# Hybrid encoder step: step sizes beside attention, one pool for LayerNorm and RG-LRU, gates ahead in the down stage

## The chip, the cores and the metric

One core of a Trainium2 chip runs the whole kernel. The metric is the device time of one execution in microseconds (us), a median of several. TensorE multiplies, VectorE (DVE), ScalarE (ACT) and GpSimd (POOL) do the rest, and every DMA is issued from one queue, that of SyncE (SP).

## The reference, cut to what matters

1088 frames (1024 of a new stream, 64 of a running one) go through one layer. One projection feeds four branches, their gates and four merge gates.

```
h = rms_norm(x); P = h @ w_in                       # 1088 x 1024 @ 1024 x 10248
A: RG-LRU:  conv4 -> r, i = sigmoid(block gates);  log_a = -8 r softplus(-lam)
            h_t = a_t h_{t-1} + sqrt(1 - a_t^2) (i_t x_t)
B: SSD:     conv4 -> SiLU; dt = softplus(P_dt + bias); chunked scan with decay exp(cumsum(-dt exp(a_log)))
C: conv31 over a GLU -> LayerNorm over channels -> swish
D: stick-breaking attention, 8 heads, strictly causal
u_b = branch_b * silu(gate_b);  y_b = u_b @ w_down[b];  m = sum_b sigmoid(P_merge_b) * y_b
x <- x + rms_norm(m @ w_out)
```

## The kernel before

Everything is in fp32 accuracy: each large product is three matmuls (`mm3`: high by high, high by low, low by high part), the parts made by `split` (a copy on ACT, a subtraction on DVE). `with tc.manual_schedule(engines={PE})` makes TensorE's order that of the source. The order on the other engines and on the DMA queue is set by the framework's planner: it takes what is ready by its own reckoning, the earlier in the source first, and `tc.high_priority(offset=...)` moves an instruction ahead. In a queue nothing passes a waiting instruction.

The stages, in order of time:

1. Norm of x, transposes to `hh`, `hl` (both parts of h, transposed, kept in SBUF).
2. Attention, L526 to L571: 4 head pairs `c`, 17 `Unit`s each (`scores`, `turn`, `output`). Between units `feed.step` puts pieces of projection chunks (`proj`: 24 matmuls into a PSUM tile `pj`, then `evac`). In the last head pair the chunks left in `extra` (15 pieces) are fed, at `want = 18 * (k + 1) // 16` pieces by unit k, so the last units have none.
3. T stage, L575 to L674. The gates of branch C (`spill`, 12 pieces, evacuated by ACT at L599) fill TensorE. Beside it the sums and differences of quarters of h are made for a Strassen-like product: `g11`..`g21` by eight `G.tensor_tensor` (POOL, L616), then differences on DVE (L618 to L624) and splits into `quad` 5, 6, 7 (and 4 at the end, over `hh`, `hl`). The step sizes of B are in this stage too: 48 matmuls with 16 columns of weights (L634), nine transposes (L640), softplus (L257) and the decay sums (L655).
4. Strassen stage, L720: 20 `Pair`s of chunks, 7 products each in `ORDER = (1, 2, 6, 5, 7, 3, 4)`, 24 matmuls each into PSUM tiles `bank` (6). After each product `next(side)` lets one step of the side chain issue its work: `layer_norm` (27 steps), then `lru` (35), then `ssd` (77), 139 of the 140 steps. Each opens its pool at its start, in the place of the one that it follows. `lru` handles 8 pieces (4 channel blocks, 2 halves of 544 frames): 6 + 6 matmuls a step apart, four sigmoids, Exp, Tanh, Sqrt, a scan, a split `uah`, `ual` and its stores. `uah` shares the memory of `ga`, the result of Exp, and `ual` that of `lg_t`, the gate that is loaded.
5. Down stage, L1114 to L1186: for each branch in `order = (3, 0, 2, 1)` and each of 8 column blocks d, pieces of 12 matmuls go to `pj3` (6 tiles), and DVE multiplies by the merge gate (L1165). The gate is loaded from `mgs` and goes through a sigmoid on ACT (`load_gate`, L1133). In the source the loads of the first operand (L1106, four) come first, then the first weights, then the second operand's four loads, then the eight gates. The tiles `mt` are placed ahead of the gates' tiles.
6. Output product, norm and store.

PSUM is one pool per stage group: `ps` (stages 1 to 3), `ps2` (4), `ps3` (5, 6). A pool with `reuse_waits="tile"` waits for the tiles that lay where its own tiles lie; without it, a new pool waits for all of the pools whose place it takes. The three PSUM pools have it not.

Of the kernel before, what the change touches and what calls it, by code (L numbers as in the profile page):

```python
# [8 lines left out]
FT = mybir.dt.float32  # L9
FR = mybir.dt.float32r  # L10
# [35 lines left out]
def encoder_step(ctx, tc, x, prm, win, wdt, wdn, wout, lwa, lwx, ckT, cv_, ssd0, npre, npost, dtb, alog, dskip,  # L46
# [10 lines left out]
    ps = ps1.enter_context(tc.tile_pool(name="ps", bufs=1, space=PSUM))  # L57
# [467 lines left out]

    feed.add(cf_sig(0), cf_glu(0), k_chunk(0), q_chunk(0), g_chunk(0))  # L526
# [7 lines left out]
    NU = 17  # L534
    units[0].scores()
    for m, u in enumerate(units):
        c, k = divmod(m, NU)
        if k == 0:
            if c < 3:
                feed.add(cf_sig(c + 1), v_chunk(c + 1) if c else extra.pop(0), extra.pop(0), g_chunk(c + 1), cf_glu(c + 1), extra.pop(0))  # L540
            else:
                feed.add(*extra)
            fed = 0
# [3 lines left out]
        want = min(18, 18 * (k + 1) // (NU - 1))  # L547
# [19 lines left out]
        else:  # L567
# [7 lines left out]
    wdr = const.tile([128, 8, 8], FT, name="wdr")  # L575
    dma(wdr, wdt)
    wd2 = const.tile([128, 8, 16], FR, name="wd2")
    S.activation(wd2[:, :, 0:8], wdr, AF.Copy)
    V.tensor_sub(wd2[:, :, 8:16], wdr, wd2[:, :, 0:8].bitcast(FT))
    dtb_t = const.tile([128, 8], FT, name="dtb_t")  # L580
    dma(dtb_t, ap(dtb, 0, [[0, 128], [1, 8]]))
    a_t = const.tile([128, 8], FT, name="a_t")
    dma(a_t, ap(alog, 0, [[0, 128], [1, 8]]))
    S.activation(a_t, a_t, AF.Exp)
    dsk = const.tile([128, 4], FT, name="dsk")
    for h in range(2):
        dma(dsk[h * 64:h * 64 + 64, :], ap(dskip, h, [[0, 64], [2, 4]]))
# [15 lines left out]
    feed.add(*(spill(C_CG + c, cg_d[:, c]) for c in range(4)))  # L603
    feed.step(1)
# [21 lines left out]
    feed.step(2)  # L626


    dtr = tmp.tile([16, T], FT, name="dtr")
    for i, (t0, n) in enumerate(SPL):  # L630
        p = pg()
        for k in range(8):
            for q, hx in enumerate((hh, hl)):
                PE.matmul(p[:16, :n], wd2[:, k, :], hx[:, k, t0:t0 + n], start=k == 0 and q == 0, stop=k == 7 and q == 1)  # L634
        S.activation(dtr[:, t0:t0 + n], p[:16, :n], AF.Copy)
    feed.step(3)
    pd = pg()
    for i in range(9):
        r = 128 if i < 8 else 64
        PE.transpose(pd[:r, i * 16:i * 16 + 16], dtr[:, i * 128:i * 128 + r], ident[:16, :16])  # L640
    pd3 = pd[:, :144].rearrange("p (i c) -> p i c", c=16)
    zb = tmp.tile([128, 9, 8], FT, name="zb", bufs=1)
    V.memset(zb, 0.0)
    for r, i0, i1 in ((128, 0, 8), (64, 8, 9)):
        V.tensor_tensor(zb[:r, i0:i1], pd3[:r, i0:i1, 0:8], dtb_t[:r, None, :].to_broadcast([r, i1 - i0, 8]), op=OP.add)
        V.tensor_tensor(zb[:r, i0:i1], pd3[:r, i0:i1, 8:16], zb[:r, i0:i1], op=OP.add)
    dt = dq.tile([128, 9, 8], FT, name="dt", bufs=1)
    V.tensor_copy(dt, softplus(tmp, zb, [9, 8], "spd"))
    adt = dq.tile([128, 9, 8], FT, name="adt", bufs=1)
    V.scalar_tensor_tensor(adt, dt, -1.0, a_t[:, None, :].to_broadcast([128, 9, 8]), op0=OP.mult, op1=OP.mult)  # L650
    V.memset(adt[64:128, 8, :], 0.0)
    feed.step(4)
# [25 lines left out]
    ps = ps2.enter_context(tc.tile_pool(name="ps2", bufs=1, space=PSUM))  # L678
# [84 lines left out]

    def layer_norm():
        lnp = ExitStack()
        ln = lnp.enter_context(tc.tile_pool(name="ln", bufs=1, side="right", reuse_waits="tile"))

# [13 lines left out]
        for q in range(4):  # L781
# [32 lines left out]
    def lru():
        p4 = ExitStack()
        lp = p4.enter_context(tc.tile_pool(name="lru", bufs=1, side="right", reuse_waits="tile"))
        nl = lp.tile([128, 4], FT, name="nl")
        V.tensor_scalar(nl, P("lam", 0, 4), -1.0, None, op0=OP.mult)
        sp = softplus(lp, nl, [4], "spl")
        lm8 = lp.tile([128, 4], FT, name="lm8")  # L820
        lp4 = lp.tile([128, 4], FT, name="lp4")
        V.tensor_scalar(lm8, sp, -8.0, None, op0=OP.mult)
        V.tensor_scalar(lp4, sp, 4.0, None, op0=OP.mult)
        hfin = lp.tile([128, 2, 4], FT, name="hfin")
        raws = [lp.tile([128, 128], FT, name=f"bd{e}") for e in "ax"]
        for r_ in raws:
            G.memset(r_, 0.0)

        def load(c, j):
            t = slice(j * HT, j * HT + HT)  # L830
            if j == 0:
                self.bd = []
                for r_, src, e in zip(raws, (lwa, lwx), "ax"):
# [3 lines left out]
                    self.bd.append([lp.tile([128, 128], FR, name=f"bd{e}{f}") for f in "hl"])  # L837
                    split(*self.bd[-1], r_)
            xc = lp.tile([128, HT], FT, name="xl", bufs=2)
            dma(xc, xl_d[:, c, t])  # L840
            xh, xl = (lp.tile([128, HT], FR, name=f"xg{f}") for f in range(2))
            split(xh, xl, xc)
            return xc, xh, xl

        class self:
            pass
        todo = [(c, j) for c in range(4) for j in range(2)]
        nxt = load(0, 0)
        yield from wait(3)
        for m, (c, j) in enumerate(todo):  # L850
            t = slice(j * HT, j * HT + HT)
            xc, xh, xl = nxt
            g = lp.tile([128, HT], FT, name="lg_t")
            dma(g, lg_d[:, c, t])
            gr = lp.tile([128, HT], FT, name="gr", bufs=2)
            gx = lp.tile([128, HT], FT, name="gx", bufs=2)
            for t0 in (0, QT):
                for dst, w, bias in ((gr, self.bd[0], P("ba", c)), (gx, self.bd[1], P("bx", c))):
                    p = pg()[:, :QT]
                    mm3(p, w[0], w[1], xh[:, t0:t0 + QT], xl[:, t0:t0 + QT], True, True)  # L860
                    S.activation(dst[:, t0:t0 + QT], p, AF.Sigmoid, bias=bias)
                if t0 == 0:
                    yield
            if m < 7:
                nxt = load(*todo[m + 1])
            ga = lp.tile([128, HT], FT, name="ga")
            S.activation(ga, gr, AF.Exp, scale=lm8[:, c:c + 1])  # L867
            S.activation(gr, gr, AF.Tanh, scale=lp4[:, c:c + 1])
            S.activation(gr, gr, AF.Sqrt)
            V.tensor_tensor(gx, gx, xc, op=OP.mult)  # L870
            V.scalar_tensor_tensor(gr, ga, 1.0, gr, op0=OP.add, op1=OP.mult)
            V.tensor_tensor(gx, gx, gr, op=OP.mult)
            hp_, hs = hfin[:, 0, c:c + 1], hfin[:, 1, c:c + 1]
            n = TP - HT if j else HT
            V.tensor_tensor_scan(gx[:, :n], ga[:, :n], gx[:, :n], hp_ if j else 0.0, OP.mult, OP.add)
            V.tensor_copy(hp_, gx[:, n - 1:n])
            if j:
                V.tensor_tensor_scan(gx[:, n:], ga[:, n:], gx[:, n:], P("h0", c), OP.mult, OP.add)
                V.tensor_copy(hs, gx[:, HT - 1:HT])
            V.tensor_tensor(gx, gx, g, op=OP.mult)  # L880
            uh = lp.tile([128, HT], FR, name="uah", tag="ga")
            ul = lp.tile([128, HT], FR, name="ual", tag="lg_t")
            split(uh, ul, gx)
            dma(uh_d[0][:, c, t], uh.bitcast(FT))
            dma(ul_d[0][:, c, t], ul.bitcast(FT))
            yield from wait(3)
        for i in range(2):
            dma(lh_o[i], hfin[:, i, :])
        p4.close()


    def ssd():
# [136 lines left out]
        yield from wait(3)  # L1029
# [244 lines left out]
```

## Time and profile before

| | us |
|---|---|
| median of 3 runs | 1481.57 (1480.87 to 1486.69) |
| profiled execution, its own time | 1485.84 |
| its span, first to last instruction | 1484.1 |
| TensorE busy with matmuls | 1421.5 |
| VectorE, ScalarE, GpSimd busy | 1065.9, 672.6, 266.4 |
| mean granted TensorE clock | 0.982 |

A row of the waits says which instruction waited for which, in total, how often and the longest. A row of the windows says how long each engine was busy in a stretch, with the instructions in brackets, and the granted TensorE clock as a share of 2.4 GHz (0.50 is 1.2 GHz).

### The profile page before, as it was taken

To read this page: it belongs to the slowest core of one execution; us is meant where nothing else is said; L and a number is where in the kernel's file an instruction comes from. 1 tells how busy PE (TensorE), PEld (TensorE's weight loads), DVE (VectorE), ACT (ScalarE), POOL (GpSimd) and SP (SyncE) were. 2 spreads that over 40 slices of the span, in tenths; PEclk is the share of its full clock that TensorE was granted. 3 is DMA by queue.
4 is the path that set the end of the run, shared out by engine and by line. 5 is a ranking of instruction groups with operands and counts; after the bars stand their busy time and mean duration, and the time that the engine had idled before them with its cause. 6 is when DMAs were issued, how large, how long until landed. Compare 5 with 4: busy or idle time off the path is not lost.

```text
span 1484.1 us, 25423 instructions
## 1 busy us (share of the span) xinstructions
PE 1421.5 (96%) x9901; PEld 1359.9 (92%) x9901; DVE 1065.9 (72%) x1628; ACT 672.6 (45%) x1225; POOL 266.4 (18%) x245
## 2 busy tenths in 40 slices
PE   8999999999999999899979989999999799999997
PEld 7999999999999998799979989999999799999885
DVE  6299799789779986847967775777877336668433
ACT  6224544544453464345769762443444242234211
POOL 0003221230231224513213231321211000000000
PEclk9999999999999999999999999999999989999999
DMA  6232213213213133134645444334343985643322
GB/s 216 69 88 65 71 49 90 94 41 101 76 55 93 52 102 107 53 109 146 207 138 175 156 139 140 124 108 154 121 132 97 334 336 170 242 149 101 112 86 71
DMA packets 113336, 184.45 MB, mean 124 GB/s; under 512 B 22080, under 2 KB 70080, under 8 KB 112704
## 3 DMA queue, kind: packets, MB, share of 16 engines
q1 hardware_dynamic: 113216, 182.82, 37.9%
q8 instruction: 78, 1.28, 0.4%
q14 instruction: 42, 0.34, 0.1%
HBM read 118.00 MB, written 60.59 MB: 120 GB/s over the span
## 4 chain that ended last, share of the span: by engine, by line
PE 38%; DVE 8%; DMA 5%; ACT 4%; issue 2%; SPq 0%; DVEq 0%; ACTq 0%
PE bank L736 16%; PE pj L109 6%; PE pj L111 6%; PE pj L110 6%; DVE w_lo L236 2%; DMA uh<-uoh 1%; DMA w_raw<-in_wout_dram 1%; DMA uh<-uah 1%; ACT w_hi L235 1%; DMA sga<-mgs 1%; PE pg L927 1%; DVE r L743 1%; PE pg L980 1%; DVE lnx L802 1%; ACT L867 1%
## 5 line engine op out<-in xcount | busy, mean ns | idle before, releaser
L110 PE MATMUL pj<-hl,w_hi 128*128 128x384 f32 (+4 forms) x1184 | 384.3, 325 | 1.1 <-DVE hl L232 1.1
L109 PE MATMUL pj<-hh,w_hi 128*128 128x384 f32 (+4 forms) x1088 | 354.4, 326 | 6.0 <-ACT t L599 4.6
L111 PE MATMUL pj<-hh,w_lo 128*128 128x384 f32 (+4 forms) x1088 | 351.9, 323 | 0.0
L110 PEld LDWEIGHTS pj<-hl,w_hi 128*128 128x128 f32 x1184 | 224.8, 190 | 3.1 <-DVE hl L232 2.0
L109 PEld LDWEIGHTS pj<-hh,w_hi 128*128 128x128 f32 x1088 | 206.0, 189 | 8.4 <-ACT t L599 4.7
L111 PEld LDWEIGHTS pj<-hh,w_lo 128*128 128x128 f32 x1088 | 205.5, 189 | 0.3
L736 PE MATMUL bank<-hh,w_hi 128*128 128x272 f32 x640 | 190.2, 297 | 1.8 <-ACT t L599 1.8
L736 PE MATMUL bank<-hh,w_lo 128*128 128x272 f32 x640 | 185.7, 290 | 0.0
L736 PE MATMUL bank<-hl,w_hi 128*128 128x272 f32 x640 | 185.7, 290 | 0.0
L250 DVE SCALAR_TENSOR_TENSOR cvo<-cbuf,p_t,cvo 128x1118 f32<-128x1118 f32 x120 | 165.5, 1379 | 1.8
L736 PE MATMUL bank<-Th,w_hi 128*128 128x272 f32 x480 | 142.8, 298 | 0.5 <-ACT r L740 0.5
L736 PE MATMUL bank<-Th,w_lo 128*128 128x272 f32 x480 | 139.5, 291 | 0.0
L736 PE MATMUL bank<-Tl,w_hi 128*128 128x272 f32 x480 | 139.3, 290 | 0.0
L736 PEld LDWEIGHTS bank<-hh,w_hi 128*128 128x128 f32 x640 | 121.9, 190 | 3.5 <-ACT t L599 2.0
L736 PEld LDWEIGHTS bank<-hl,w_hi 128*128 128x128 f32 x640 | 121.8, 190 | 0.6
L736 PEld LDWEIGHTS bank<-hh,w_lo 128*128 128x128 f32 x640 | 121.6, 190 | 0.0
L475 POOL TENSOR_SCALAR_AFFINE_SELECT fb<-fb 128x128 f32<-128x128 f32 (+1 forms) x72 | 40.1, 557 | 449.1 <-ACT fb L470 329.5
L478 DVE TENSOR_TENSOR_SCAN fb<-fb,ones 128x128 f32<-128x128 f32 (+8 forms) x68 | 90.1, 1326 | 27.8 <-POOL fb L475 27.7
L102 DVE TENSOR_TENSOR w_lo<-w_raw,w_hi 128x1024 fp32r<-128x1024 f32 x56 | 70.8, 1264 | 46.8 <-ACT w_hi L101 46.3
L740 ACT ACTIVATE r<-bank 128x272 f32<-128x272 f32 x160 | 62.0, 390 | 91.7 <-PE bank L736 91.4
L101 ACT ACTIVATE w_hi<-w_raw 128x1024 fp32r<-128x1024 f32 x56 | 59.3, 1060 | 78.5 <-PE pj L110 70.6
L736 PEld LDWEIGHTS bank<-Th,w_hi 128*128 128x128 f32 x480 | 91.7, 191 | 2.6 <-issue 1.2
(347 smaller groups left out, 2994.3 us busy)
## 6 DMA issues: line engine op xcount, KB each, us to landing
w_raw<-in_win_dram SPq DMA_DIRECT2D x80, 512.0 KB, 4.0
mgs<-r SPq DMA_DIRECT2D x64, 272.0 KB, 2.2
sga<-mgs SPq DMA_DIRECT2D x32, 544.0 KB, 4.4
w_raw<-in_wdn_dram SPq DMA_DIRECT2D x16, 512.0 KB, 4.7
xt<-in_x_dram SPq DMA_DIRECT2D x8, 512.0 KB, 9.5
xbc<-xc SPq DMA_DIRECT2D x8, 512.0 KB, 2.6
xb<-xbc SPq DMA_DIRECT2D x8, 512.0 KB, 4.9
w_raw<-in_wout_dram SPq DMA_DIRECT2D x8, 512.0 KB, 4.2
```

Source lines behind the costliest of these rows:

```text
L101: S.activation(hi, r3, AF.Copy)
L102: V.tensor_sub(lo, r3, hi.bitcast(FT))
L109: PE.matmul(out, ah, bh, start=first, stop=False)
L110: PE.matmul(out, ah, bl, start=False, stop=False)
L111: PE.matmul(out, al, bh, start=False, stop=last)
L235: S.activation(hi, src, AF.Copy)
L236: V.tensor_sub(lo, src, hi.bitcast(FT))
L250: V.scalar_tensor_tensor(out[:, :n], b[:, i:i + n], w[:, i:i + 1], out[:, :n], op0=OP.mult, op1=OP.add)
L475: G.affine_select(t_[s, 1024 - w:1024], t_[s, 1024 - w:1024], pattern=[[-1, w]], compare_op=OP.is_gt, fill=fill, base=0, channel_multiplier=1)
L478: V.tensor_tensor_scan(F[:, rev], F[:, rev], ones[:, 0:1].to_broadcast([128, n]), 1.0, OP.mult, OP.mult)
L736: PE.matmul(p, a_[:, k], b_[:, k, s], start=new and k == 0 and z == 0, stop=k == 3 and z == 2, skip_group_check=True)
L740: S.activation(R[to][:, s], p, self.last if j == 4 else AF.Copy)
```

## The change

- The step sizes' matmuls and transposes become a piece of work, `step_sizes`, fed last in the last head pair of the attention. The pace there is 17 pieces instead of 18, of 19 that there are; the rest follows behind the last unit. The small loads around it stand earlier in the source.
- Their softplus runs at the start of the T stage at high priority, together with the softplus of the RG-LRU's `lam` (76 columns instead of 72, and 4 later).
- The eight additions of quarters go from GpSimd to VectorE.
- The three PSUM pools get `reuse_waits="tile"`.
- LayerNorm and RG-LRU share a pool `ln`. The RG-LRU's first loads are issued in LayerNorm's third and its first split in LayerNorm's fourth quarter. Its tiles take LayerNorm's slots. `uah`, `ual` no longer share a slot with `ga` and the loaded gate. The split of the next piece (`prepare`) stands behind a piece's end instead of ahead of its Exp.
- The side chain's steps: LayerNorm 25, RG-LRU 32, SSD 79 (five steps instead of three between its first loads and its first matmuls).
- Down stage: the second weights are loaded with the first, and from then on one ahead; four gates are loaded before the second operand and take the lowest place of the freed memory, the other four before it too.

```diff
-    ps = ps1.enter_context(tc.tile_pool(name="ps", bufs=1, space=PSUM))
+    ps = ps1.enter_context(tc.tile_pool(name="ps", bufs=1, space=PSUM, reuse_waits="tile"))
...
-    def weights(src):
+    def fetch(src):
         raw = wp.tile([128, 1024], FT, name="w_raw", bufs=2)
         dma(raw, src)
+        return raw
+
+    def weights(src, raw=None):
+        raw = fetch(src) if raw is None else raw
...
+    def step_sizes():
+        dtr = cp.tile([128, T], FT, name="dtr", tag="sb", bufs=1)
+        dts.append(dtr)
+        yield
+        for t0, n in SPL:
+            p = pg()
+            for k in range(8):
+                for q, hx in enumerate((hh, hl)):
+                    PE.matmul(p[:16, :n], wd2[:, k, :], hx[:, k, t0:t0 + n], start=k == 0 and q == 0,
+                              stop=k == 7 and q == 1)
+            S.activation(dtr[:16, t0:t0 + n], p[:16, :n], AF.Copy)
+            yield True
+        pd = dts[0] = pg()
+        for i in range(9):
...
+        yield True
...
-                feed.add(*extra)
+                feed.add(*extra, step_sizes())
...
-        want = min(18, 18 * (k + 1) // (NU - 1))
+        want = min(18 - (c == 3), (18 - (c == 3)) * (k + 1) // (NU - 1))
...
+    with tc.high_priority(offset=ATT_PRIO):
+        V.memset(zb, 0.0)
...
+        sp = softplus(tmp, zl, [76], "spd")
...
-            G.tensor_tensor(g, hh[:, ks, t].bitcast(FT), hl[:, ks, t].bitcast(FT), op=OP.add)
+            V.tensor_tensor(g, hh[:, ks, t].bitcast(FT), hl[:, ks, t].bitcast(FT), op=OP.add)
...
+            if q == 2:
+                lru.fetch(0, 0)
+            if q == 3:
+                lru.prepare(0, 0)
...
-            yield from wait(3)
-        lnp.close()
...
+            yield from wait(3 if q < 3 else 1)
...
+            xc = self.xc[c, j] = ln.tile([128, HT], FT, name="xl", tag=("xl", "lnh")[j])
+            dma(xc, xl_d[:, c, j * HT:j * HT + HT])
+
+        def prepare(self, c, j):
+            self.xg = ln.tile([128, 2, HT], FR, name="xg", tag="lnq")
+            split(self.xg[:, 0], self.xg[:, 1], self.xc[c, j])
...
+                eg = ln.tile([128, 2, HT], FT, name="eg", tag="lng")
+                ga, g = eg[:, 0], eg[:, 1]
+                dma(g, lg_d[:, c, t])
+                rx = ln.tile([128, 2, HT], FT, name="rx", tag="lnx", bufs=2)
...
+                uh = ln.tile([128, HT], FR, name="uah", tag="lns", bufs=2)
+                ul = ln.tile([128, HT], FR, name="ual", tag="lns", bufs=2)
+                split(uh, ul, gx)
+                dma(uh_d[0][:, c, t], uh.bitcast(FT))
+                dma(ul_d[0][:, c, t], ul.bitcast(FT))
+                yield from wait(2)
+                if m < 7:
+                    self.prepare(*todo[m + 1])
+                yield
...
-        yield from wait(3)
+        yield from wait(5)
...
-    nwd = weights(wdn[order[0], 0])
+    downs = [(b, e) for b in order for e in range(4)]
+    nwd = weights(wdn[downs.pop(0)])
+    raw = fetch(wdn[downs.pop(0)])
...
-    gates = [load_gate(order[0], d) for d in range(8)]
+    gates = [load_gate(order[0], d) for d in range(4)]
+    mp = ctx.enter_context(tc.tile_pool(name="mp", bufs=1, reuse_waits="tile"))
+    mt = [mp.tile([128, T], FT, name=f"m{d}") for d in range(8)]
+    gates += [load_gate(order[0], d) for d in range(4, 8)]
+    us.append(Operand(order[1], [t_[:, k, thi] for t_ in (hh, hl) for k in (k0, k1)]))
...
-                if i == 0 and d % 2 and (d < 7 or bi < 3):
-                    nwd = weights(wdn[b, d // 2 + 1] if d < 7 else wdn[order[bi + 1], 0])
+                if i == 0 and d % 2 and raw is not None:
+                    nwd = weights(None, raw)
+                    raw = fetch(wdn[downs.pop(0)]) if downs else None
```

## Rows read from the trace of the kernel before

**Rows 1.** The page: busy time of each engine, share of the span, instructions.

```profile
PE 1421.5 (96%) x9901; PEld 1359.9 (92%) x9901; DVE 1065.9 (72%) x1628; ACT 672.6 (45%) x1225; POOL 266.4 (18%) x245
```

**Rows 2.** TensorE's waits, whole span: waiter, releaser, us in total, times, longest.

```profile
PE pj L109 <- DVE m L1165: 9.0, 1, 9.0
PE pg L109 <- ACT xg L235: 8.2, 1, 8.2
PE pj L109 <- ACT t L599: 4.6, 1, 4.6
PE pg L927 <- DVE lt L917: 4.4, 1, 4.4
PE pg L980 <- DVE xdt L952: 4.2, 4, 1.5
...
PE pg L109 <- ACT gr L861: 3.0, 1, 3.0
PE pg L490 <- DVE beta L479: 2.3, 1, 2.3
...
PE bank L736 <- ACT t L599: 1.8, 1, 1.8
...
PE pj L109 <- ACT rs__12699 L1017: 1.4, 1, 1.4
```

**Rows 3.** Windows, lower clock: length; PE, PEld, DVE, ACT, POOL busy; PEclk; DMA share, GB/s.

```profile
577.90:581.40 3.50, 3.50 (x26) 3.17 (x27) 3.01 (x5) 1.39 (x3) 0.69 (x2) 0.51 0.22 77
618.90:625.80 6.90, 5.07 (x16) 5.07 (x17) 6.87 (x7) 5.35 (x8) 0.00 (x0) 0.51 0.15 56
649.60:653.00 3.40, 3.40 (x17) 3.40 (x17) 0.90 (x2) 0.40 (x1) 2.34 (x2) 0.50 0.68 184
755.40:762.30 6.90, 3.78 (x15) 3.47 (x16) 1.52 (x6) 3.53 (x6) 0.00 (x0) 0.51 0.43 132
851.00:854.40 3.40, 3.38 (x15) 3.28 (x15) 3.37 (x9) 2.80 (x7) 0.55 (x1) 0.50 0.32 121
888.60:895.40 6.80, 6.14 (x21) 5.11 (x22) 3.85 (x8) 2.17 (x4) 0.00 (x0) 0.50 1.08 281
1185.50:1195.80 10.30, 5.68 (x25) 5.69 (x26) 2.62 (x7) 6.09 (x6) 0.00 (x0) 0.50 1.03 411
```

**Rows 4.** The 48 matmuls of L634 alone, in the T stage: us, PE busy, PEld busy.

```profile
595.60:603.60 8.00, 7.98 (x48) 4.44 (x47) 1.00 0.06 7
```

**Rows 5.** Timeline of the DMA queue, early: start, us, line, names.

```profile
24.81 1.32 SPq L587 DMA_DIRECT2D dsk<-in_dskip_dram  x2
```

**Rows 6.** Timelines of VectorE and GpSimd in the T stage.

```profile
591.75 3.62 DVE L618 TENSOR_TENSOR g<-g,g 128x1088 f32<-128x1088 f32 x1
...
617.86 1.29 DVE L618 TENSOR_TENSOR g<-g,g 128x1088 f32<-128x1088 f32 x1 [4.88 <-POOL g L616]
...
611.80 6.03 POOL L616 TENSOR_TENSOR g<-hh,hl 128x1088 f32<-128x1088 f32 x2
```

**Rows 7.** Timeline of the DMA queue at the RG-LRU's start.

```profile
754.56 0.58 SPq L840 DMA_DIRECT2D xl<-xls  x1
```

**Rows 8.** ScalarE's waits, 837 to 873 us.

```profile
ACT L867 <- DMA uh<-uah: 7.0, 2, 3.9
```

**Rows 9.** Timeline of TensorE, then ScalarE, around one RG-LRU hand-over.

```profile
793.18 0.29 PE L111 MATMUL pg<-xg,bdxl 128*128 128x272 f32 x1
...
802.34 0.29 PE L109 MATMUL pg<-xg,bdah 128*128 128x272 f32 x1
...
804.25 0.49 ACT L861 ACTIVATE gr<-pg,p_t 128x272 f32<-128x272 f32 x1
805.85 0.66 ACT L235 ACTIVATE uah<-gx 128x544 fp32r<-128x544 f32 x1 [1.12 <-DVE gx L880]
```

**Rows 10.** Window of one Exp, Tanh and Sqrt with their two table loads (columns as above).

```profile
795.43:800.23 4.80, 4.80 (x41) 4.80 (x40) 2.68 (x4) 4.72 (x6) 1.64 (x1) 1.00 0.70 234
```

**Rows 11.** The chain that ended last, start of the down stage.

```profile
1178.06 10.39 DMA sga<-mgs
```

More of the change, by code (lines that the diff above doesn't have):

```diff
@@ L524, in output @@
             dma(ul_d[3][:, c, i * 128:i * 128 + m], ul[:, :m].bitcast(FT))
+    wdr = const.tile([128, 8, 8], FT, name="wdr")
+    dma(wdr, wdt)
+    wd2 = const.tile([128, 8, 16], FR, name="wd2")
+    S.activation(wd2[:, :, 0:8], wdr, AF.Copy)
+    V.tensor_sub(wd2[:, :, 8:16], wdr, wd2[:, :, 0:8].bitcast(FT))
+    dtb_t = const.tile([128, 8], FT, name="dtb_t")
+    dma(dtb_t, ap(dtb, 0, [[0, 128], [1, 8]]))
+    a_t = const.tile([128, 8], FT, name="a_t")
+    dma(a_t, ap(alog, 0, [[0, 128], [1, 8]]))
+    S.activation(a_t, a_t, AF.Exp)
+    dsk = const.tile([128, 4], FT, name="dsk")
+    for h in range(2):
+        dma(dsk[h * 64:h * 64 + 64, :], ap(dskip, h, [[0, 64], [2, 4]]))
+    dts = []
+    def step_sizes():
[12 more added lines that the diff above has]
+        for i in range(9):
+            r = 128 if i < 8 else 64
+            PE.transpose(pd[:r, i * 16:i * 16 + 16], dtr[:16, i * 128:i * 128 + r], ident[:16, :16])
+        yield True
     feed.add(cf_sig(0), cf_glu(0), k_chunk(0), q_chunk(0), g_chunk(0))
@@ L571, in encoder_step @@
             u.output(None)
+    pd = dts[0]
     p1.close()
     p2.close()
[L575 to L587, printed above, removed]
     a1 = ExitStack()
@@ L603, in encoder_step @@
     feed.add(*(spill(C_CG + c, cg_d[:, c]) for c in range(4)))
+    pd3 = pd[:, :144].rearrange("p (i c) -> p i c", c=16)
+    zl = tmp.tile([128, 76], FT, name="zb", bufs=1)
+    zb = zl[:, :72].rearrange("p (i c) -> p i c", c=8)
+    dt = dq.tile([128, 9, 8], FT, name="dt", bufs=1)
+    lm8 = dq.tile([128, 4], FT, name="lm8")
+    lp4 = dq.tile([128, 4], FT, name="lp4")
+    adt = dq.tile([128, 9, 8], FT, name="adt", bufs=1)
+    with tc.high_priority(offset=ATT_PRIO):
+        V.memset(zb, 0.0)
+        for r, i0, i1 in ((128, 0, 8), (64, 8, 9)):
+            V.tensor_tensor(zb[:r, i0:i1], pd3[:r, i0:i1, 0:8], dtb_t[:r, None, :].to_broadcast([r, i1 - i0, 8]), op=OP.add)
+            V.tensor_tensor(zb[:r, i0:i1], pd3[:r, i0:i1, 8:16], zb[:r, i0:i1], op=OP.add)
+        V.tensor_scalar(zl[:, 72:76], P("lam", 0, 4), -1.0, None, op0=OP.mult)
+        sp = softplus(tmp, zl, [76], "spd")
+        V.tensor_copy(dt, sp[:, :72].rearrange("p (i c) -> p i c", c=8))
+        V.tensor_scalar(lm8, sp[:, 72:76], -8.0, None, op0=OP.mult)
+        V.tensor_scalar(lp4, sp[:, 72:76], 4.0, None, op0=OP.mult)
+        V.scalar_tensor_tensor(adt, dt, -1.0, a_t[:, None, :].to_broadcast([128, 9, 8]), op0=OP.mult, op1=OP.mult)
+        V.memset(adt[64:128, 8, :], 0.0)
     feed.step(1)
@@ L625, in encoder_step @@
         t4.append((kd, g21))
[L626 to L652, printed above, removed]
+    feed.step(8)
     pa = pg()
@@ L677, in encoder_step @@
     ps2 = ExitStack()
-    ps = ps2.enter_context(tc.tile_pool(name="ps2", bufs=1, space=PSUM))
+    ps = ps2.enter_context(tc.tile_pool(name="ps2", bufs=1, space=PSUM, reuse_waits="tile"))
     def pg():
@@ L809, in layer_norm, with __init__, fetch @@
             dma(ul_d[2][:, :, t], gw.bitcast(FT))
-            yield from wait(3)
-        lnp.close()
[L814 to L830, printed above, removed]
+            yield from wait(3 if q < 3 else 1)
+    class Lru:
+        def __init__(self):
+            self.raws = [ln.tile([128, 128], FT, name=f"bd{e}") for e in "ax"]
+            for r_ in self.raws:
+                V.memset(r_, 0.0)
+            self.hfin = ln.tile([128, 2, 4], FT, name="hfin")
+            self.xc = {}
+        def fetch(self, c, j):
             if j == 0:
-                self.bd = []
-                for r_, src, e in zip(raws, (lwa, lwx), "ax"):
+                for r_, src in zip(self.raws, (lwa, lwx)):
                     for h in range(2):
@@ L836, in load @@
                         dma(r_[s, s], src[s, c])
-                    self.bd.append([lp.tile([128, 128], FR, name=f"bd{e}{f}") for f in "hl"])
+                self.bd = []
+                for e, r_ in zip("ax", self.raws):
+                    self.bd.append([ln.tile([128, 128], FR, name=f"bd{e}{f}") for f in "hl"])
                     split(*self.bd[-1], r_)
-            xc = lp.tile([128, HT], FT, name="xl", bufs=2)
-            dma(xc, xl_d[:, c, t])
-            xh, xl = (lp.tile([128, HT], FR, name=f"xg{f}") for f in range(2))
@@ L842, in load @@
[L842 to L848, printed above, removed]
-        yield from wait(3)
[L850 to L886, printed above, removed]
@@ L892, in ssd @@
+    lru = Lru()
     def ssd():
@@ L1057, in chains @@
         yield from layer_norm()
-        yield from lru()
+        yield from lru.run()
         yield from ssd()
@@ L1124, in pg @@
         return ps.tile([128, 512], FT, name="pg3", bufs=2)
-    us.append(Operand(order[1], [t_[:, k, thi] for t_ in (hh, hl) for k in (k0, k1)]))
-    mp = ctx.enter_context(tc.tile_pool(name="mp", bufs=1, reuse_waits="tile"))
-    mt = [mp.tile([128, T], FT, name=f"m{d}") for d in range(8)]
     sgp = ctx.enter_context(tc.tile_pool(name="sgp", bufs=1, reuse_waits="tile"))
@@ L1182, in encoder_step @@
             wo1.append(sgp.tile([128, 1024], FR, name=f"wp{d}", tag=f"sga{d}"))
-            raw = wp.tile([128, 1024], FT, name="w_raw", bufs=2)
-            dma(raw, wout[d])
+            ro = fetch(wout[d])
             for w, e in ((wo0[:, d], 0), (wo1[d], 1)):
-                split(w[:, 0:512], w[:, 512:1024], raw[:, e * 512:e * 512 + 512])
+                split(w[:, 0:512], w[:, 512:1024], ro[:, e * 512:e * 512 + 512])
     wo = [[wo0[:, d] for d in range(8)], wo1]
```

43 lines of the change are left out of this document (36 added, 7 removed).

## The prediction

> **What bounds the kernel now.** I read the page first: TensorE is busy 1421.5 us of a span of 1484.1 us [rows 1], and its order is fixed by hand, so the time is its work, its idle time and what a lower clock adds. The 20 us windows over the whole span come next: TensorE is full nearly everywhere, and short of full at the start and at seven places from 575 us on. Then TensorE's waits say who ended each idle time [rows 2]: eight waits at these seven places are 9.0 + 8.2 + 4.6 + 4.4 + 3.0 + 2.3 + 1.8 + 1.4 = 34.7 us. Last, windows cut to where the granted clock fell: seven stretches at 0.50 to 0.51, that is 1.2 GHz [rows 3]. Each begins during one of these waits or within 2.5 us after it; none follows the four waits for `xdt`. Work done at 1.2 GHz takes twice as long, so each stretch gives back half of its busy time if the wait ahead of it goes: (3.50 + 5.07 + 3.40 + 3.78 + 3.38 + 6.14 + 5.68) / 2 = 15.5 us. The reader is to see that 50.2 us hang on these eight waits, and that a saving on another engine counts only where it ends one of them.
>
> **The change part by part.**
>
> Step sizes beside attention. The 48 matmuls take 8.0 us wherever they stand [rows 4], so moving them saves nothing by itself. But two of their three groups (5.4 us) come where TensorE stood 2.3 us waiting for `beta` of the last unit but one [rows 2], because the chunks had run out; with pieces 17 to the head pair, the last chunk piece comes one unit later as well. So 2.3 us of wait and 1.75 us of clock (half of 3.50, [rows 3]) go: 4.1 us. The lower bound is nothing, if the unit's chain gets later by as much. The small loads cost nothing in their new place in the source, because they already ran at 24.8 us [rows 5], before attention: the planner takes what is ready. That row also tells how to read the other moves: for engines other than TensorE, a place in the source is a rank, not a time.
>
> Additions on VectorE, softplus first. In the T stage TensorE waits 4.6 us for the evacuation at L599, which stands on ACT behind a split that waits for L618 on DVE, which waits for GpSimd. Two GpSimd additions take 6.03 us; L618 takes 3.62 us beside GpSimd and 1.29 us without [rows 6]. After the change DVE has 22 such operations, 22 x 1.29 = 28.4 us, besides some 7 us of softplus and three subtractions of weights; TensorE has 12 pieces of 24 matmuls, 48 us at the pace of [rows 4], until it needs the results. Eight additions cost DVE 10.3 us and take 24 us (8 x 3.0) out of its chain. So 4.6 us and 2.5 us of clock go: 7.1 us; the lower bound is nothing, if ACT waits for DVE all the same. The Trainium skill speaks against this edit: its page Perfetto Trace Analysis, section Optimizing Scalar/DVE Operations, says that moving operations between GpSimd and VectorE might not help, since the two share a read port. By that rule the 7.1 us would stay; but the rows of this trace that show the sharing (3.62 against 1.29 us) are rows in which both engines worked at once, and here one of them loses its work.
>
> PSUM by bank. Two openings of a PSUM pool make TensorE wait for the last reader of the pool before: 1.8 us at the first Strassen matmul, with 1.7 us of clock (half of 3.40), and 1.4 us at the first down matmul, for a square root of the last norm [rows 2, 3]. With waits by tile the first tile needs only its own old readers, done some microseconds earlier. The weights were ready in both places. Sum 4.9 us; lower bound nothing.
>
> LayerNorm and RG-LRU in one pool. At the hand-over TensorE waits 8.2 us for the split of the first `xl` [rows 2]; its load was issued at 754.6 us [rows 7], because the new pool opened behind LayerNorm's end. With the loads two quarters and the split one quarter ahead, 8.2 us and 1.9 us of clock go: 10.1 us. Inside the RG-LRU, Exp waited 7.0 us in two waits for the store of `uah` in whose slot it writes [rows 8]; the late ACT queue then gave TensorE's 3.0 us wait for `gr`, with 1.7 us of clock. The new slots take this away: 4.7 us. At the start of SSD TensorE waits 4.4 us for `lt`; its step now stands 8 products behind the last RG-LRU matmuls instead of 6; three products lie between the two matmuls of [rows 9], 9 us, so two are 6 us more, so 4.4 and 3.1 us go: 7.5 us.
>
> Down stage. The first gate landed 10.39 us after its issue at 1178.1 us, behind the 4.4 MB of the second operand [rows 11]. TensorE had filled the six tiles by 1181.1 us and stood 9.0 us [rows 2]. Four gates ahead of the second operand are 2.2 MB, some 5.4 us at the 411 GB/s of that place [rows 3], on memory that frees at the third product of the last pair, some 20 us before the stage starts. So the first gate is there before the first piece ends, and 9.0 + 2.8 = 11.8 us go. The early weights I count at nothing: no wait for the down stage's weights is among the long ones [rows 2].
>
> What stays: the first 41 us, a wait of 2.3 us at 516 us, the four for `xdt` (4.2 us), the last 7.7 us.
>
> The sum: 4.1 + 7.1 + 4.9 + 10.1 + 4.7 + 7.5 + 11.8 = 50.2 us.
>
> What comes new. The weakest edit is `prepare`. Before, the split of the next `xl` ranked ahead of Exp; now it ranks behind Exp, Tanh, Sqrt and `uah`. From the last matmul of a piece to the first of the next are 9 us (793.2 to 802.3 us, [rows 9]). Exp, Tanh and Sqrt with two table loads take 4.8 us of ACT [rows 10]; estimated, the products' own work there takes some 2 us, and the split (0.66 us, as that of `uah`, [rows 9]) and its subtraction as long each: 8.1 us, which just fits. The planner does pass waiting work: the sigmoid of the next piece, later in the source, ran at 804.25 us ahead of `uah` at 805.85 us [rows 9]. So the bounds for each of seven hand-overs are nothing and 4.9 us (the split behind `uah`: 805.85 + 2 x 0.66 against 802.3 us); being near the lower, I take 0.7 us, 5 us in all. Exp of the first piece now writes where LayerNorm's last part was, and must wait for that store, until some 752 us against about 742 us; TensorE doesn't wait for Exp, but ACT's queue may: 2 us. Another 2 us for waits that the closed ones had hidden. So 50.2 - 9 = 41 us.
>
> The profiled execution took 1485.84 us: it would come to 1444.8 us. It lies 4.3 us over the median, so the median goes from 1481.57 to about 1441 us.
>
> **The rivals.**
>
> 1. The hand-over inside the RG-LRU becomes the bound: the split does stand behind `uah` on ACT. Price 7 x 4.9 = 34 us, and 1.7 us of clock each (half of 3.4) makes 46 us: 50.2 - 46 - 4 leaves nothing, 1477 to 1487 us. This is the way to no gain or a loss; it decides from some 4 us a hand-over on. For it speaks the rank, against it rows 9. Chance 0.10 in full, 0.15 for half of it, about 1460 us.
> 2. The additions save nothing, as the cited rule has it: DVE, with some 39 us of work in a stage of 48 us, holds ACT's splits and with them the evacuation. Then 7.1 us stay: 1448 us. Against it: with three tiles `pj` ACT's queue may be two pieces late, 8 us. Chance 0.10.
> 3. The gates still come late, because the DMA queue issues in order and the second weights ahead of them wait for their slot, or a store of SSD's last norm holds the queue. 11.8 us stay: 1453 us. Against it: SSD ends three products earlier now. Chance 0.10.
>
> **How the numbers follow.** The forecast has 0.55: all eight waits go but for some 9 us; its own range is 1431 (nothing new) to 1452 us. With rivals 2, 3 and half of rival 1 it reaches to 1465 us; the full rival 1 (0.10) and the edges are left out, so 1430 to 1465 us. A measurement of this kernel can tell about 0.5%, 7.4 us, from no change: faster than 1474 us is all but the full rival 1, 0.90; of that, 0.05 falls within the 0.5% and 0.05 above.
>
> **What would show it.** TensorE's waits of the changed kernel without L599, L618's chain, `xg`, `lt`, `gr` and L1165, and without 1.2 GHz stretches at these places; matmuls of `step_sizes` between the last two units; the first gate landed before TensorE's first down piece ends. Wrong would be waits for `xg` at most hand-overs (rival 1), one for L599's evacuation (rival 2), one for L1165 of several microseconds (rival 3), or a large new wait for anything else.

## The result, and the profile after

The changed kernel takes 1465.13 us (median of 4 runs, 1463.11 to 1467.54) beside 1482.37 us of the kernel before: a ratio of 0.988, with a 95% interval of 0.985 to 0.991. It is 17 us faster; 41 were predicted, to 1441 us. The profiled execution took 1467.54 us (span 1465.8 us), 18.3 us less than that of before.

The page, busy time of the engines as in [rows 1]:

```profile
PE 1415.9 (97%) x9901; PEld 1355.2 (92%) x9901; DVE 1061.7 (72%) x1622; ACT 682.1 (47%) x1230; POOL 236.0 (16%) x235
```

TensorE's waits over the whole span, to be laid beside [rows 2] (L113 of after is L109 of before, L239 is L235, L876 is L861):

```profile
PE pg L113 <- ACT xg L239: 7.7, 2, 7.2
PE pj L113 <- ACT w_hi L105: 7.5, 1, 7.5
PE pg L113 <- ACT rx L876: 6.1, 3, 2.9
...
PE pg L114 <- DVE xg L240: 3.1, 4, 1.2
```

Six of the eight waits of [rows 2] are gone: those for `beta` at L490, for both evacuations of the T stage, for the root of the last norm, for `lt`, and for the merge gate's product. The wait for `xg` stayed; the one for `gr` (now `rx`) grew; and there is a new one, 7.5 us for `w_hi`, at the place in the down stage where TensorE stood for `m` before.

The windows of the low clock from the RG-LRU on, columns as in [rows 3]:

```profile
729.30:732.70 3.40, 3.40 (x17) 3.40 (x16) 1.30 (x2) 2.67 (x5) 0.00 (x0) 0.50 0.01 3
742.90:753.20 10.30, 6.29 (x26) 5.99 (x27) 6.85 (x8) 7.72 (x10) 1.96 (x2) 0.50 0.53 177
1183.20:1193.50 10.30, 5.63 (x23) 5.31 (x24) 2.80 (x3) 6.56 (x6) 0.00 (x0) 0.50 1.02 388
```

Of the seven stretches of [rows 3], those in the T stage, at the first Strassen product and at SSD's start have no successor. The RG-LRU and the down stage have their stretches still, each begun during or just behind one of the waits above; half of the busy time in them is lost again.

What became of the sum, wait and half of the low stretch together:

| term | predicted gain, us | in the two profiles, us |
|---|---|---|
| step sizes | 4.1 | 4.1 |
| additions, softplus | 7.1 | 7.1 |
| PSUM by bank | 4.9 | 4.9 (but see e6) |
| hand-over and RG-LRU | 10.1 + 4.7 - 9 new | -6.1: 15.7 before (8.2 + 0.9 + 3.0 and 3.6 of clock), 21.8 after (7.7 + 6.1 + 3.1 and 4.9 of clock) |
| start of SSD | 7.5 | 7.5 |
| down stage | 11.8 | 1.0: 11.8 before, 10.8 after (7.5, 0.4 for `w_lo`, 2.8 of clock) |
| sum | 41 | 18.5; the profiled executions differ by 18.3 |

That the two agree so closely is partly luck, because what lies outside the table nearly cancels: the waits for `xdt` (now `xdd`) fell from 4.2 to 2.3 us, while this execution of the changed kernel was at a low clock from 38 to 48 us, where no edit is (mean granted clock 0.66; some 3 us lost, where the one of before lost some 1.5 us from 10 to 16 us). The term of the step sizes is read from these profiles alone: no run undoes that edit.

Two terms failed, by 12 and 11 us. These are their places.

**The RG-LRU's start.** ScalarE's timeline from the root of LayerNorm's last quarter to the split of the RG-LRU's second piece (start, length, line, operation; in brackets the idle time ahead and what ended it):

```profile
721.19 0.49 ACT L815 ACTIVATE lnr<-pg,eps_t 128x272 f32<-128x272 f32 x1
...
722.74 1.28 ACT L876 ACT_TABLE_LOAD   x1
...
724.53 1.28 ACT L771 ACT_TABLE_LOAD   x1
...
728.30 1.28 ACT L826 ACT_TABLE_LOAD   x1
...
737.90 1.10 ACT L239 ACTIVATE lnh<-lnx 128x1088 fp32r<-128x1088 f32 x1
...
744.08 1.28 ACT L881 ACT_TABLE_LOAD   x1 [2.24 <-DMA ul<-lnl]
745.37 0.75 ACT L881 ACTIVATE eg<-rx,lm 128x544 f32<-128x544 f32 x1
746.03 0.66 ACT L239 ACTIVATE xg<-xl 128x544 fp32r<-128x544 f32 x1
```

The first RG-LRU matmuls run at 721.3 us, just as LayerNorm's last quarter takes its root; its SiLU and its split are still ahead. The RG-LRU's sigmoids (L876) therefore alternate on ScalarE with SiLUs of the gates (L771) and of LayerNorm (L826) and with roots, and each change is a table load: eight between 719.9 and 740 us, 8 x 1.28 = 10.3 us, where the kernel before had six in the 48 us from 712 to 760. And the second piece takes memory that LayerNorm's last quarter still uses. The DMA queue there:

```profile
739.03 0.53 SPq L831 DMA_DIRECT2D uh<-lnh  x1
740.39 0.51 SPq L832 DMA_DIRECT2D ul<-lnl  x1
...
742.42 1.17 SPq L855 DMA_DIRECT2D xl<-xls  x2
```

The second `xl` lies in the slot of `lnh` and is loaded only when the store of `lnh` has landed; Exp, ahead of the split of that `xl`, writes in the slot of `lnl` and waits 2.24 us for the other store. So from the root at 721.19 to the end of the split at 746.69 there are 25.5 us. TensorE comes for the second piece at 739.56 us, 18.4 us after the root, and stands the other 7.1 us (measured: 7.18).

**The down stage.** The chain that ended last, from the last Strassen product on (start, length, what):

```profile
1160.48 11.07 DMA sga<-mgs
...
1171.58 1.12 ACT sga L1152
...
1174.09 12.14 DMA w_raw<-in_wdn_dram
...
1186.32 1.06 ACT w_hi L105
```

The gates do come early: the first one's sigmoid ran at 1160.94 us, and the eighth landed at 1171.55 us, before TensorE had filled its tiles. But the second operand's four loads were issued at 1161.0 to 1171.1 us, and the third weights, 0.5 MB, behind them at 1174.09 us. They landed at 1186.24 us; TensorE had stood since 1179.89 us.

### The profile page after: what moved, and what is told of

It reads as the page before. It is cut to its first block, busy times and chain, and to the rows that moved or that the text cites. A ratio compares the mean times of both kernels' runs of the same rounds, so it can differ in the third digit from the quotient of the medians.

```text
span 1465.8 us, 25422 instructions
## 1 busy us (share of the span) xinstructions
PE 1415.9 (97%) x9901; PEld 1355.2 (92%) x9901; DVE 1061.7 (72%) x1622; ACT 682.1 (47%) x1230; POOL 236.0 (16%) x235
## 3 DMA queue, kind: packets, MB, share of 16 engines
q8 instruction: 78, 1.28, 0.4%
## 4 chain that ended last, share of the span: by engine, by line
PE 51%; DVE 5%; ACT 4%; DMA 3%; issue 2%; SPq 0%; DVEq 0%; ACTq 0%
PE bank L755 21%; PE pj L115 8%; PE pj L113 8%; PE pj L114 8%; DVE w_lo L240 1%; DMA w_raw<-in_wdn_dram 1%; DMA sga<-mgs 1%; PE pg L999 1%; ACT w_hi L239 1%; PE pg L512 1%; PE pg L555 1%; PE pg L946 1%; DMA ul<-uol 1%; PE pg L494 0%; PE pg L955 0%
## 5 line engine op out<-in xcount | busy, mean ns | idle before, releaser
L113 PE MATMUL pj<-hh,w_hi 128*128 128x384 f32 (+4 forms) x1088 | 355.2, 326 | 7.8 <-ACT w_hi L105 7.5
L113 PEld LDWEIGHTS pj<-hh,w_hi 128*128 128x128 f32 x1088 | 206.7, 190 | 10.5 <-ACT w_hi L105 7.8
```

Source lines behind the costliest of these rows:

```text
L113: PE.matmul(out, ah, bh, start=first, stop=False)
```

## The experiments

Each is the changed kernel with one edit, timed in rounds beside the kernel before. The kernel before was at 1484.75 us beside e1 to e4, at 1481.79 beside e5 to e8, at 1481.21 beside e9 to e11, at 1480.84 beside e12; the ratios (with 95% intervals) are what compares best. The changed kernel's is 0.988 (0.985 to 0.991). Differences from the changed kernel in us are differences of medians, not of runs side by side.

**e1, the second operand later.**

```diff
-    us.append(Operand(order[1], [t_[:, k, thi] for t_ in (hh, hl) for k in (k0, k1)]))
...
+            if bi == 0 and d == 2:
+                us.append(Operand(order[1], [t_[:, k, thi] for t_ in (hh, hl) for k in (k0, k1)]))
```

> The changed kernel, but the second operand's four loads (4.4 MB) are issued when the third column block of the first branch begins, not ahead of the stage. Theory (the third weights land 12.1 us after their issue because the second operand and eight gates are ahead of them in the DMA queue): the wait of 7.5 us for w_hi at 1180 us and the 3.0 us of lower clock behind it go, about 1455 us against 1465. Rival (the weights wait for their slot or for ScalarE's queue): no change, 1463 to 1467 us.

Measured: 1456.84 us, 0.981 (0.980 to 0.983), 8.3 us less than the changed kernel (by the ratios 9.8). The wait for `w_hi` is gone, and this window over its place, columns as in [rows 3], has the clock at 1.00:

```profile
1175.00:1195.00 20.00, 18.59 (x148) 18.36 (x147) 7.65 (x15) 6.45 (x6) 0.00 (x0) 1.00 0.96 347
```

In its DMA queue the third weights now stand ahead of the second operand (issue, length, line):

```profile
1163.25 0.43 SPq L96 DMA_DIRECT2D w_raw<-in_wdn_dram  x1
...
1168.02 0.58 SPq L1125 DMA_DIRECT2D hh<-uh  x1
```

The cause in the down stage is shown: one place in the order of the queue.

**e2, the split ahead of Exp.**

```diff
                 if m < 7:
                     self.fetch(*todo[m + 1])
+                    self.prepare(*todo[m + 1])
...
-                yield from wait(2)
-                if m < 7:
-                    self.prepare(*todo[m + 1])
-                yield
+                yield from wait(3)
```

> The changed kernel, but the split of the next xl stands ahead of Exp in the source again. Theory of the rank (the split came behind Exp in ScalarE's queue): the wait of 7.2 us for xg at 740 us, its 3.3 us of lower clock and the waits of 3.1 us for the second half of xg go, about 1452 us. Rival, the slot (Exp waits for LayerNorm's last store, whatever stands behind it, and holds evacuations): at most 3 us are gained, 1462 us or more.

Measured: 1464.81 us, 0.987 (0.986 to 0.989), no difference. The 7.2 us stay (738.95 to 746.12 us); the four waits for the second part of `xg` shrink from 3.1 to 0.2 us in all, and those for `rx` grow from 6.1 to 7.4. So the rank of the split, the weakest edit by the prediction, is not by itself what costs at this place: the load of `xl` behind the store of `lnh` is still there.

**e3, Exp's result in memory of its own.**

```diff
-                eg = ln.tile([128, 2, HT], FT, name="eg", tag="lng")
-                ga, g = eg[:, 0], eg[:, 1]
+                ga = ln.tile([128, HT], FT, name="ga")
+                g = ln.tile([128, HT], FT, name="lg_t", tag="lng")
```

> The changed kernel, but Exp writes to a tile of its own; the loaded gate keeps LayerNorm's slot. Theory of the slot: Exp no longer waits for LayerNorm's last store, and most of the 7.2 us and 3.3 us at 740 us go, about 1456 us. Theory of the rank: only ScalarE's wait of 2.2 us for the store goes, the split still stands behind Exp, 1461 to 1464 us.

Measured: 1464.56 us, 0.986 (0.985 to 0.988); the wait is 7.88 us. Exp's slot alone isn't it either.

**e4, the two pools and the chain of before** (with the moved softplus and all other edits kept).

```diff
-            yield from wait(3 if q < 3 else 1)
+            yield from wait(3)
+        lnp.close()
...
+    def lru():
+        p4 = ExitStack()
+        lp = p4.enter_context(tc.tile_pool(name="lru", bufs=1, side="right", reuse_waits="tile"))
...
-        yield from wait(5)
+        yield from wait(3)
```

> The changed kernel with LayerNorm and RG-LRU in pools of their own as before, three steps ahead of SSD's first matmuls, the softplus of lam staying where the change put it. If the shared pool cost as much as it gave (waits and clock of the RG-LRU 21.8 us after, 15.7 us before with the hand-over from LayerNorm, and 7.5 us at SSD's start before): about the same as the changed kernel, 1463 to 1468 us, less 1 or 2 us for the softplus that is gone from the hand-over. If it gained as predicted (22 us) and the loss is elsewhere: about 1485 us.

Measured: 1467.55 us, 0.989 (0.987 to 0.990). TensorE's waits of e4 bring back those of [rows 2]:

```profile
PE pg L113 <- ACT xg L239: 8.1, 1, 8.1
...
PE pg L939 <- DVE lt L929: 5.4, 1, 5.4
...
PE pg L113 <- ACT gr L873: 3.5, 1, 3.5
```

So the shared pool with its new slots, the earlier start and the two more steps ahead of SSD are together worth about 2 us, which is not clear of noise (the intervals overlap): what SSD's start gave, the RG-LRU took.

**e5, the additions on GpSimd again.**

```diff
-            V.tensor_tensor(g, hh[:, ks, t].bitcast(FT), hl[:, ks, t].bitcast(FT), op=OP.add)
+            G.tensor_tensor(g, hh[:, ks, t].bitcast(FT), hl[:, ks, t].bitcast(FT), op=OP.add)
```

> The changed kernel with the eight additions of quarters on GpSimd again. By the prediction's step TensorE's wait for the evacuation in the T stage (4.6 us) and its 2.5 us of lower clock come back: about 1472 us against 1465. Rival (the move saves nothing, because GpSimd and VectorE hinder each other or because the softplus alone did it): 1463 to 1467 us.

Measured: 1476.53 us, 0.9965 (0.9954 to 0.9976), 11.4 us more than the changed kernel. Its waits, its two low stretches (columns as in [rows 3]), and GpSimd's and VectorE's timeline:

```profile
PE pj L113 <- ACT t L625: 8.4, 2, 4.6
```

```profile
611.90:618.70 6.80, 5.53 (x21) 5.54 (x22) 5.19 (x8) 1.60 (x3) 3.03 (x1) 0.50 0.41 130
625.60:632.40 6.80, 4.23 (x13) 4.23 (x14) 6.80 (x11) 4.16 (x6) 0.00 (x0) 0.50 0.08 29
```

```profile
592.02 14.64 POOL L661 TENSOR_TENSOR g<-hh,hl 128x1088 f32<-128x1088 f32 x5
```

```profile
597.09 3.62 DVE L663 TENSOR_TENSOR g<-g,g 128x1088 f32<-128x1088 f32 x1 [4.97 <-POOL g L661]
```

An addition takes 2.93 us on GpSimd, and VectorE stands 4.97 us for it; in the changed kernel the eight take VectorE 11.2 us, 1.40 each. Two evacuations come late instead of one. The Trainium skill's caution that such a move might not help (page Perfetto Trace Analysis, section Optimizing Scalar/DVE Operations) is not borne out here, where the move is worth these 11.4 us: GpSimd loses the work, and VectorE no longer stands for it.

**e6, PSUM pools that wait for whole pools.** The three `reuse_waits="tile"` of `ps`, `ps2`, `ps3` taken out.

> The changed kernel with the three PSUM pools waiting for whole pools again. By the prediction's step 1.8 us, 1.7 us of clock and 1.4 us come back: about 1470 us. Rival (SSD ends three products earlier now, so the down stage's first matmul no longer meets the last norm's square root): 3.5 us or less, 1465 to 1468.5 us.

Measured: 1466.79 us, 0.991 (0.989 to 0.992). 1.48 us of wait come back at the first Strassen matmul (635.41 us) and 0.49 us at the first down matmul, with no low stretch behind them. The interval overlaps that of the changed kernel, so a gain from this edit is not shown in the time.

**e7, `xl` in two slots of its own.**

```diff
-            xc = self.xc[c, j] = ln.tile([128, HT], FT, name="xl", tag=("xl", "lnh")[j])
+            xc = self.xc[c, j] = ln.tile([128, HT], FT, name="xl", bufs=2)
```

> The changed kernel, but xl has two slots of its own; no half lies in the slot of LayerNorm's last part lnh. The split of xl at 746 us is held twice by LayerNorm's stores: its load waits for the store of lnh, and ScalarE reaches it behind Exp, which waits for the store of lnl. If both hold it, this edit alone changes little: TensorE's wait of 7.2 us stays above 5 us, 1462 to 1465 us. Rival (the load is what holds it): the wait and its clock go, about 1455 us.

Measured: 1463.81 us, 0.990 (0.987 to 0.992). The 7.2 us become 3.00 us for ScalarE's half of the split and 3.06 us for VectorE's.

**e8, e7 with the split ahead of Exp** (the edits of e7 and e2).

> As the one before, with the split of the next xl ahead of Exp in the source as well. If the load and the place behind Exp both hold the split, the wait of 7.2 us and its 3.3 us of lower clock go, and the waits for the second half of xg (3.1 us): about 1453 us. Rival (ScalarE's table loads, eleven between 719 and 751 us, hold everything there): the wait stays above 4 us, 1461 us or more.

Measured: 1466.32 us, 0.990 (0.989 to 0.992). TensorE's waits between 700 and 860 us:

```profile
PE pg L113 <- ACT rx L876: 10.3, 6, 3.7
PE pg L114 <- DVE xg L240: 3.4, 2, 3.1
PE pg L113 <- ACT xg L239: 3.1, 1, 3.1
```

With the memory free and the split first, two waits of 3.1 us are still there: ScalarE, with the same eight table loads, has no gap from 715.7 to 738 us, and reaches the split at 737.41. This is what that run's rival had named, and it accounts for the first of the two. The second is VectorE's: its half of the split stands behind two subtractions of weights, which take 3.42 us while GpSimd is busy (the hardware section has the same pair at 1.28 us). e7 has the same two rows. VectorE's timeline:

```profile
737.66 3.42 DVE L240 TENSOR_TENSOR w_lo<-w_raw,w_hi 128x512 fp32r<-128x512 f32 x2
741.01 0.71 DVE L240 TENSOR_TENSOR xg<-xl,xg 128x544 fp32r<-128x544 f32 x1
```

And the waits for `rx` grew from 6.1 to 10.3 us, so TensorE's waits from 700 to 860 us are as long in all as in the changed kernel.

**e9, the RG-LRU three steps later**, and **e10, five steps later**, at the product where it started before.

```diff
-            yield from wait(3 if q < 3 else 1)
+            yield from wait(3 if q < 3 else 4)
```

In e10 the 4 is a 6.

> The changed kernel, but the RG-LRU's first matmuls come three products later, behind the last product of the pairs that need a SiLU; SSD's five steps of lead stay. Theory (the early start mixes sigmoids with the SiLUs and roots of the pairs and of LayerNorm; ScalarE loads 8 tables of 1.28 us between 719 and 740 us, before 3 in as long): the waits of 2.6 and 7.2 us there shrink to under 4 us together, with 2 to 4 us of clock: about 1457 us. Rival (the hand-over is bound by the stores of LayerNorm's last part, whose slots the RG-LRU takes): no change beyond 2 us.

> As the one before, but five products later, at the same product as in the kernel before. Theory of the early start: both waits go, and with them 5 us of clock: 1450 to 1454 us, the gain of the shared pool that was predicted at the hand-over; SSD then ends a step later than the last product, which costs less than 2 us. Rival (the stores): 1461 us or more.

Measured: e9 1457.38 us, 0.983 (0.981 to 0.986), 7.8 us less than the changed kernel (the intervals just touch), the time that was expected. The two waits all but go: 0.57 us is left at 732 us, and the second piece comes without a wait at 742.66 us. But two new ones are at the third piece, from 756 us on: TensorE stands 2.64 us for ScalarE's half of the split and 3.26 us for VectorE's. e10 took 1446.00 us, 0.975 (0.973 to 0.978), 19 us less than the changed kernel and 4 us below the expected range. TensorE's waits of e10 between 700 and 860 us, all of them:

```profile
PE pg L114 <- DVE xg L240: 2.2, 2, 1.7
PE pg L113 <- ACT rx L876: 1.2, 3, 0.8
PE bank L755 <- ACT r L759: 0.6, 1, 0.6
PE pg L813 <- DVE lns L790: 0.3, 1, 0.3
```

ScalarE's timeline of e10, from the same root to the same split:

```profile
719.62 0.49 ACT L815 ACTIVATE lnr<-pg,eps_t 128x272 f32<-128x272 f32 x1
...
729.99 1.11 ACT L239 ACTIVATE lnh<-lnx 128x1088 fp32r<-128x1088 f32 x1
...
735.43 1.28 ACT L876 ACT_TABLE_LOAD   x1
...
742.80 0.64 ACT L239 ACTIVATE xg<-xl 128x544 fp32r<-128x544 f32 x1
```

The split of LayerNorm ends 11.5 us after the root instead of 17.8, with no sigmoid between, and the chain to the end of the piece's split takes 23.8 us. TensorE has its first matmul of the second piece at 748.3 us, 28.7 us after the root. The chain fits, by 4.9 us.

Waits and half of the low clock in the RG-LRU, 21.8 us in the changed kernel, are 5 us here: 3.4 us of waits for `xg` and `rx`, and 1.6 us for one low stretch from 792.4 to 795.9 us. That is 17 of the 19 us; 2 more are the down stage's, where the wait for `w_hi` is 4.8 us instead of 7.5.

e4 and e10 start the RG-LRU at the same product. e4, without the shared pool, the new slots and the steps ahead of SSD, has 0.989; e10, with them, has 0.975. So these edits are worth some 20 us where the start stays.

**e11, e10 with e1's edit.**

> The changed kernel with the RG-LRU five products later and the second operand's loads behind the third weights. The two faults are in different stages, so the gains add: 8.3 us (measured for the operand alone) and 11 to 15 us: 1442 to 1446 us, the time that was predicted. If they are not independent, over 1450 us.

Measured: 1438.72 us (1438.62 to 1440.43), 0.971 (0.969 to 0.973), the best of all: 42.5 us under the kernel before. It is 3 us below the expected range. The gains nearly add: 8.3 + 19.1 = 27.4 us by the two alone, 26.4 together (by the ratios 28.8 and 24.9; in e10 the wait that e1's edit ends is only 4.8 us). Its two longest waits of TensorE, and its page row:

```profile
PE pz L461 <- ACT beta L475: 3.4, 2, 2.2
PE pg L999 <- DVE xdt L971: 3.2, 4, 1.4
```

```profile
PE 1406.6 (98%) x9901; PEld 1346.8 (94%) x9901; DVE 1064.7 (74%) x1622; ACT 674.3 (47%) x1226; POOL 239.7 (17%) x235
```

Its mean granted clock is 0.997 (0.987 in the changed kernel), and the same 9901 matmuls take 9.3 us less; some 3 us of that are the changed kernel's low stretch from 38 to 48 us, where no edit is.

**e12, fewer table loads at the same start** (this kernel leaves out the SiLU of the gates of A and B).

```diff
-    pairs = [stored(C_LG, c, lg_d, AF.Silu) for c in (0, 2)] + [stored(C_SZ, c, sz_d, AF.Silu) for c in (0, 2)]
+    pairs = [stored(C_LG, c, lg_d, AF.Copy) for c in (0, 2)] + [stored(C_SZ, c, sz_d, AF.Copy) for c in (0, 2)]
```

> The changed kernel in which the four evictions of the gates of A and of B (pairs 0 to 3) are plain Copies in place of SiLUs: the same instructions at the same places, and the SiLU of those gates is left out of the computation. The start of the RG-LRU and the slots stay as they are. Theory (the table loads that mixed functions put into ScalarE's queue delay LayerNorm's last split and all that hangs on it between 720 and 746 us): fewer table loads between 719 and 740 us, the 2.6 us wait of TensorE at 726 us goes, the 7.2 us one shrinks below 4 us, and the time is 1455 to 1459 us. Rival (the late stores and slots of LayerNorm's last part alone, whatever ScalarE runs): the 7.2 us wait stays above 6 us, and the time is 1462 us or more.

Measured: 1463.81 us, 0.987 (0.986 to 0.989). The theory's first half came (three table loads in place of eight between 719 and 740 us, and the 2.6 us wait gone), its second didn't: 6.45 us stay at 734.90 us. ScalarE's timeline:

```profile
717.17 0.49 ACT L815 ACTIVATE lnr<-pg,eps_t 128x272 f32<-128x272 f32 x1 [1.22 <-PE pg L813]
...
731.85 1.12 ACT L239 ACTIVATE lnh<-lnx 128x1088 fp32r<-128x1088 f32 x1
...
738.70 1.28 ACT L881 ACT_TABLE_LOAD   x1 [2.61 <-DMA ul<-lnl]
...
740.65 0.64 ACT L239 ACTIVATE xg<-xl 128x544 fp32r<-128x544 f32 x1
```

The chain is 24.1 us, 1.4 shorter, but TensorE, without the first wait, comes 17.7 us after the root, and stands the rest. The time and the wait are those of its rival, the late stores and slots. But e7 and e8, which free the slots, keep as much. So neither the table loads nor the slots are the single cause; either way alone leaves 6 to 6.5 us.

## Why the prediction was off

- **What was read rightly.** That TensorE's waits and the half clock behind them set the time: worked out so, the changed kernel gains 18.5 us beside 18.3 between the profiled executions (closer than it deserves, as said above), and e5 loses 8.4 + (5.53 + 4.23) / 2 = 13.3 us beside 11.6 between the spans, 1477.4 and 1465.8. Step sizes (by the profiles alone) and the start of SSD came out in full. Of the SSD term e4 shows that it belongs to the steps and the pool: undone, 5.4 us are back.
- **"LayerNorm and RG-LRU in one pool", 10.1 + 4.7 us: the step that failed.** The prediction said that loads two quarters and a split one quarter ahead would end the 8.2 us. They did, for the first piece. It passed over what its own count of steps does to the start: 25 for LayerNorm in place of 30 by its waits (its last wait went from 3 to 1, the RG-LRU's opening wait of 3 was dropped), so the RG-LRU starts five products, some 15 us, earlier. What was late next was the second piece, whose chain through LayerNorm's last quarter takes 25.5 us where TensorE gives 18.4. The prediction had seen that Exp "must wait for that store" and put 2 us on it; the place was right, but not that the next split stands behind Exp and that its own load waits for the other store. e2, e3, e7 and e12 take single links out, e8 two, and none gains anything measurable; e10 gives the chain its time back and gains 19 us. The prices were near right: at the old start the edits are worth some 20 us (e4 against e10), where the sum had 10.1 + 4.7 + 7.5 = 22.3 before the new waits. The 3.0 us for `gr` did not go either: 6.1 us for `rx` came in its place, 2.6 us of it at the early start and 2.9 us at 785 us; e10 has 1.2 us in all. What holds the one at 785 us, no run shows.
- **Rival 1 (a hand-over in the RG-LRU becomes the bound)** came in a form that it didn't name: not seven hand-overs through the rank of the split, which e2 refutes, but above all one, through the stage before. Its half-sized time, about 1460 us, was nearest the result, by luck of the number. (In e9, where ScalarE makes the third piece's split at 758.33 us, behind Exp, Tanh and Sqrt, one hand-over may be late in the rival's way; no run tests that.)
- **"Down stage", 11.8 us: the step "so the first gate is there before the first piece ends" held, the line "the early weights I count at nothing" failed.** No wait for weights was in [rows 2] because the gates held TensorE first. With the gates in front, the third weights were late next, behind the 4.4 MB of the second operand. The wait moved and kept its size; e1 ends it. Rival 3 had the right price (1453 us by itself) and the wrong transfer.
- **PSUM, 4.9 us: mis-sized.** e6 gives 1.5 + 0.5 us. So the 1.7 us of clock and most of the second wait don't come back with this edit undone; that other edits ended them is likely, but not shown.
- **Additions, 7.1 us: mis-sized the other way.** Undone alone they cost 11.4 us: in e5 a second evacuation comes late, in a stage into which the softplus had been moved too; that the softplus is why is not shown. Rival 2 is refuted.
- The forecast of 1441 us was that of a kernel in which both failed steps work. e11 is that kernel, and took 1438.72 us. That it comes within 3 us is partly luck: the additions gave 4.3 us more than forecast, PSUM some 3 us less, and the 9 us of new waits were not seen as such.

What stays open: how the 7.2 us divide between table loads, memory and VectorE's queue. Table loads and memory were each taken away without the other and left some 6 us, with memory gone half of it VectorE's; a kernel without both at the early start wasn't run. Nor is it shown why three products later end the wait at the second piece and leave one at the third, and five end both. And the wait for `w_hi` is 4.8 us in e10 where it is 7.5 us in the changed kernel; why, no run tells apart.

## What to carry to other kernels

When a stage is started earlier, count the products between its start and its second piece, and lay beside them the whole chain that the second piece hangs on: the last work of the stage before, its stores, the memory that these free, the load, the split. For a wait that is taken away, ask of the same place which transfer is late next, and read the queue's order there: what was hidden behind the old wait has no row of its own. If each link's removal alone gives nothing, the distance is what has to change.

## What the hardware showed unexpectedly

- ScalarE loads more tables when two stages that use different functions overlap than when one runs behind the other: 8 loads of 1.28 us in 20 us of the changed kernel, 3 in e10 (and 3 in e12, which has fewer functions to mix). What the five more cost by themselves is not shown: e12 is without them and gains nothing measurable. For the load alone the Trainium skill states ~1283 ns (page ScalarE: Activation LUTs, section What ACT_TABLE_LOAD costs), and this trace agrees.
- A load of 0.5 MB took 12.14 us from issue to landing behind a queue of larger ones, while 385 GB/s were moved in the same time; what is small isn't fast when it is asked for last.
- VectorE's subtractions of `w_lo` took 1.28 us a pair at 723.8 us and 3.41 us a pair at 742 us, where GpSimd was busy for 3.92 of the 4 us from 740 on. In e7 and e8 such a pair is what holds VectorE's half of the split. VectorE's timeline of the changed kernel:

```profile
723.78 1.28 DVE L240 TENSOR_TENSOR w_lo<-w_raw,w_hi 128x512 fp32r<-128x512 f32 x2
...
742.00 3.41 DVE L240 TENSOR_TENSOR w_lo<-w_raw,w_hi 128x512 fp32r<-128x512 f32 x2
```
